# One expert fewer in wide form, residual rows written in one piece, and the overflow branch moved to the end of a one-core decoder layer

## The chip, the cores and the metric

The kernel runs on one core of a Trainium2 chip. The metric is device time in microseconds of one execution; 812.87 us is the median of three runs of the kernel before (807.72, 812.87 and 814.02). The trace is that of one profiled execution.

## The reference

One layer of a decoder: 512 positions of width 1024. Three mixers (dilated window attention, a chunked state-space mixer, attention into 256 memory tokens) share an input projection, and their outputs go through `w_out`. Then a LayerNorm and a mixture of 16 experts, two for each position, and a second LayerNorm:

```python
x = _layer_norm(ALPHA * x + y, ln1_g[l], ln1_b[l])
y = _moe(x, w_router, b_router, w_gate[l], w_up[l], w_down[l])
x = _layer_norm(ALPHA * x + y, ln2_g[l], ln2_b[l])

def _moe(...):
    ...                        # top 2 experts of the best group of four; gates: 512 x 16
    for e in range(N_EXPERTS):
        h = jax.nn.silu(x @ w_gate[e]) * (x @ w_up[e])
        out = out + gates[..., e:e + 1] * (h @ w_down[e])
```

Each expert has three matrices of 1024 x 1024 in float32, 4.19 MB each, 201 MB in all.

## The kernel before

**Front.** Projections, the three mixers, `w_out` and the first LayerNorm run until about 285 us of the profiled execution. A planner (`Plan`, with `add` and `chain`) gets operations with an engine, a cost, what they depend on and a priority, and emits them in an order. The normed rows stay in four tiles `res`, one for each 128 positions.

**Experts.** The experts are computed on gathered rows only. Two kinds of places exist: HEAVY has room for 96 rows in three groups of 32, LIGHT for 64 rows in one group. Places 0 and 1 belong to experts 0 and 1; the other experts are sorted by their number of rows on the chip (`sort`), the larger ones into the HEAVY places. `PROG` is the order of the 16 places; two in a row form a pair, whose rows are gathered together by one-hot matmuls (`gather`, line 1316; for the first pair `gather_early`, line 1380) into `X`. An expert is a product with `w_gate`, a Silu on ACT, a product with `w_up`, a multiplication on VectorE, transposes (`turn`), and a product with `w_down`; down of one expert stands behind gate and up of the next. `gemm` (line 1438) loads a matrix as 8 tiles of 128 x 1024 (512 KB), each from `slot()`. A HEAVY product uses its tile in 12 matmuls as the program lists them, which the trace records as 24, a LIGHT one in 2, recorded as 4. Four accumulator banks `acc` are cycled; a HEAVY product takes two, a LIGHT one one.

**Buffers and queues.** `turns` is the order in which `slot()` hands out 33 tile buffers: raws 8, rawm 4, raw2 4, quarters 6, his 4, los 4, loopw 3, and so on again. In the trace raw stands for several of these pools, and X for two of the quarters. All weights are issued on SP's DMA queue in program order; a load waits until its buffer is no longer read and until an earlier load of the ring has landed.

**Result rows.** `xbuf` is a 512 x 1024 array in memory. It holds first the rows that the second LayerNorm adds to: SP writes the scaled bias `b1b` into it (line 988), and `residue` multiplies `res` by the scaled gain (line 1122) and adds it with accumulating DMAs on POOL's queue (line 1123). `down` then scales its result by the gate and adds it to rows of `xbuf` with an indirect accumulating DMA for each group (line 1496), 32 in all. The last two experts' down product stays on chip.

**Overflow and tail.** Rows beyond a place's room are counted in `nlefti`. `rest()` (lines 1515 to 1577) reads this count on every engine (line 1517) and, where it is above zero, runs a loop that computes them with its own weight loads into `loopw`. It stands between the last expert's up product and the tail. The tail (from 1699 on): the down weights of the last pair as 32 halves of 256 KB (line 1713), the second LayerNorm's two rows (1715), `rest()`, the transposes (1739), the product of the last pair (1749), its spreading over positions (1763), the sums with the rows read from `xbuf` (read at 1729, added at 1767), statistics, normalization (1803, 1807) and stores (1808).

Of the kernel before, what the change touches and what calls it, by code (L numbers as in the profile page):

```python
# [43 lines left out]
FIX, N_HEAVY = 2, 9  # L44
PROG = [0, 1, 2, 3, 9, 10, 4, 5, 11, 12, 6, 7, 8, 13, 14, 15]
# [62 lines left out]
def kernel(ctx, tc, x, mem, w_in, w_out, rel_bias, conv_w, conv_b, dt_bias, a_log, d_skip,  # L108
# [623 lines left out]
    plan = Plan(dict(raw=NR, hi=4, lo=4, pj=2, sc=2, tr=2, av=2, A=2, B=2, Lk=2, tb=2, mx=4, den=4, pv=2, t3=2, rT=2, rq=2, rs1=2, left=2, lt=2, xt=2,  # L732
# [243 lines left out]

    raw2 = ctx.enter_context(tc.tile_pool(name="raw2", bufs=NR4, reuse_waits="tile"))
    b1b = raw2.tile([128, 1024], F32, name="raw")
    nc.sync.dma_start(b1b, bass.AP(tensor=ln1_b[0].tensor, offset=ln1_b[0].offset, ap=[[0, 128], [1, 1024]]))
# [5 lines left out]

    def biased():
        for b in range(4):
            nc.sync.dma_start(xbuf[b * 128:(b + 1) * 128, :], b1b)
    add("SP", 0.1, biased, scale[:1])
# [46 lines left out]
    def logits_of(b, prio, deps):  # L1036

        def out():
            got["lt", b] = p2.tile([128, 128], F32, name="lt")
# [217 lines left out]
    cycle = NR * [raws] + NR2 * [rawm] + NR4 * [raw2] + NQ * ["quarter"] + 4 * [his] + 4 * [los] + NR3 * ["loopw"]  # L1257
    turns = 24 * cycle

    def slot(loop=False):  # L1260

        pool = "loopw" if loop else turns[cnt[0]]
        n, cnt[0] = turns[:cnt[0]].count(pool), cnt[0] + (not loop)
# [104 lines left out]
    def gather_early():  # L1368
# [35 lines left out]
    for b in range(4):  # L1404
        add("DVE", 0.5, lambda b=b: [place(b, pos1[:, b, z:z + 1], (HEAVY, HEAVY), z, REACH[b]) for z in range(2)], [put_at[b]], (), 402.0)

# [108 lines left out]
    def rest():  # L1515

        n_more = nc.values_load(nlefti[0:1, 0:1], min_val=0, max_val=16 * NJ)
        with tc.If(n_more > 0):
            with tc.For_i(0, n_more, 1):
# [58 lines left out]
                down(HEAVY, wrows[2], rows, turn(HEAVY, hh, X[:, :, HEAVY.slots:]), idx, gt)  # L1578

    def sort():  # L1580
# [3 lines left out]
        pc = mis("ps_c")  # L1584
        for b in range(4):
            T.matmul(pc[:, 0:16], oneb, sel[:, b, :], start=b == 0, stop=b == 3, skip_group_check=True)
        key, rank, numf = wide("key", 16), wide("rank", 16), wide("numf", 16)
        sq = pxt.tile([128, 512], F32, name="xt")[:, :256].rearrange("p (a b) -> p a b", a=16)
        V.scalar_tensor_tensor(key, pc[:, 0:16], 16.0, tie, op0=OP.mult, op1=OP.add)
        V.tensor_tensor(sq, key[:, None, :].to_broadcast([128, 16, 16]), key[:, :, None].to_broadcast([128, 16, 16]), op=OP.is_gt)  # L1590
        red(rank, sq)
        V.tensor_tensor(sq, rank[:, None, :].to_broadcast([128, 16, 16]), i16[:, :, None].to_broadcast([128, 16, 16]), op=OP.is_equal)
        V.tensor_tensor(sq, sq, i16[:, None, :].to_broadcast([128, 16, 16]), op=OP.mult)
        red(numf, sq)
        num = pf.tile([128, 16], I32, name="num")
        V.tensor_copy(num, numf)
# [52 lines left out]
        return num, numf, pos2, rem, nlefti  # L1649
# [11 lines left out]

    for i, j in enumerate(PROG):
# [17 lines left out]
        to = kind, e, idx[:, c:c + kind.groups], gt[:, c:c + kind.groups]  # L1680
        prev = lambda hh=hh, kind=kind: turn(kind, hh), lambda H, to=to: down(to[0], (w_down, to[1]), None, H, *to[2:])

        if z == 0 and i < 14:
            for b in range(4):
                for y in range(2):
                    j2 = PROG[i + 2 + y]
                    place(b, posx[:, b, j2:j2 + 1], pair_of(i + 2), y)
        elif i < 14:
# [6 lines left out]
    PT = px.tile([128, 512], F32R)  # L1695
# [7 lines left out]
    for e_ in range(2):  # L1703
        V.tensor_copy(gate2[e_ * 64:(e_ + 1) * 64], gt[e_ * 64:(e_ + 1) * 64, e_:e_ + 1])
# [137 lines left out]


# [28 lines left out]
```

## Time and profile before

| | us |
|---|---|
| runs | 807.72, 812.87, 814.02 |
| profiled execution, its own time | 808.93 |
| its span | 807.2 |
| TensorE busy | 769.5 (95%) |
| VectorE / ACT / POOL busy | 315.0 / 222.9 / 93.3 |
| DMA moved | 245.65 MB, mean 304 GB/s over the span |

The span is read by stages: the front until 285 us, the experts until 761 us, the tail from there. The shares of the whole span mix them; the rows further down are each of one stage. A row of a window gives each engine's busy time, with the number of instructions in brackets, then TensorE's granted clock as a share of full, the DMA engines' busy share and what they moved. A row of waits gives the total, the number of waits and the longest. A row of a timeline gives start and length of a run of instructions, and in square brackets the idle time before it with what ended it.

### The profile page before, as it was taken

Reading aid. Unit: us, or ns where it says so; the run is one execution under the profiler, and the core shown is the slowest. Engines: PE = TensorE matmul, PEld = TensorE weight load, DVE = VectorE, ACT = ScalarE, POOL = GpSimd, SP = SyncE. Lnnn points to the kernel's source line nnn. Section 1 sums busy time; section 2 is a strip of 40 time slices with the busy share of each in tenths; the row PEclk is TensorE's granted clock in tenths of the full one; section 3 lists DMA queues with packets and bytes.
Section 4 is the critical chain, followed back from the end, with each engine's and each line's share of the span. In section 5 each row is a group of like instructions: output and inputs, shape, how many; then the busy total and the mean of one; then the engine's idle time right before and its main releaser. Section 6 shows DMA issues by size and latency. Waiting matters only on the chain. (4 is left out here: it accounts for less than half of the span.)

```text
span 807.2 us, 20819 instructions
## 1 busy us (share of the span) xinstructions
PE 769.5 (95%) x8497; PEld 488.8 (61%) x8497; DVE 315.0 (39%) x1028; ACT 222.9 (28%) x449; POOL 93.3 (12%) x158
## 2 busy tenths in 40 slices
PE   7999999999999899999999999999999999999790
PEld 6897799787777666666654464654454556443240
DVE  5688877988957883020010020010200001010018
ACT  5667653577744330010010010010110000010112
POOL 5201200111010010010111100011100001102000
PEclk9999999999999889999999999999999999999986
DMA  8932555722574979999999999999999999999992
GB/s 290 299 95 64 80 57 75 256 79 79 189 274 162 349 201 363 417 404 412 403 405 400 393 403 399 413 404 395 400 393 413 408 404 406 408 390 406 335 343 106
DMA packets 94004, 245.65 MB, mean 304 GB/s; under 512 B 11154, under 2 KB 33240, under 8 KB 93904
## 3 DMA queue, kind: packets, MB, share of 16 engines
q1 hardware_dynamic: 86336, 232.31, 74.6%
q0 software_dynamic: 7568, 11.95, 9.0%
q8 instruction: 69, 1.13, 0.5%
q14 instruction: 31, 0.25, 0.1%
HBM read 231.46 MB, written 13.76 MB: 304 GB/s over the span
## 5 line engine op out<-in xcount | busy, mean ns | idle before, releaser
L1438 PE MATMUL acc<-raw,X 128*32 128x256 f32 (+1 forms) x2548 | 182.6, 400 | 0.0
L1438 PEld LDWEIGHTS acc<-raw,X 128*32 128x32 f32 (+1 forms) x2548 | 88.5, 113 | 76.5 <-issue 21.4
L1496 POOL DMA_INDIRECT xbuf<-y,idx x32 | 49.6, 1549 | 403.0 <-ACT y L1512 250.1
L1438 PE MATMUL acc<-raw,H 128*32 128x256 f32 (+1 forms) x1228 | 79.4, 389 | 0.0
L1512 ACT ACTIVATE y<-acc,gt 128x256 f32<-128x256 f32 (+1 forms) x23 | 11.2, 520 | 221.5 <-PE acc L1438 156.3
L1472 DVE TENSOR_TENSOR hh<-hh,acc 128x512 f32<-128x512 f32 (+1 forms) x24 | 13.4, 585 | 124.6 <-PE acc L1438 124.6
L1438 PEld LDWEIGHTS acc<-raw,H 128*32 128x32 f32 (+1 forms) x1228 | 40.6, 111 | 31.2 <-issue 6.3
L1462 ACT ACTIVATE hh<-acc 128x512 f32<-128x512 f32 (+1 forms) x25 | 12.1, 519 | 135.6 <-PE acc L1438 135.6
L1316 PEld LDWEIGHTS <-c 128*128 128x128 bf16 x768 | 31.9, 98 | 28.2 <-issue 28.1
L298 PE MATMUL pj<-hi,xh 128*128 128x256 f32 (+2 forms) x144 | 48.2, 335 | 0.4 <-ACT xh L897 0.4
L299 PE MATMUL pj<-lo,xh 128*128 128x256 f32 (+2 forms) x144 | 46.6, 324 | 0.0
L300 PE MATMUL pj<-hi,xl 128*128 128x256 f32 (+2 forms) x144 | 46.3, 321 | 0.1
L298 PE MATMUL pj<-xh,hi 128*128 128x512 f32 x112 | 45.6, 407 | 0.8 <-DVE pl L619 0.6
L300 PE MATMUL pj<-xh,lo 128*128 128x512 f32 x112 | 44.4, 397 | 0.0
L299 PE MATMUL pj<-xl,hi 128*128 128x512 f32 x112 | 44.3, 395 | 0.0
L1328 DVE TENSOR_SCALAR X<-ps_g,vcol 128x192 f32<-128x192 f32 (+2 forms) x28 | 12.1, 443 | 77.2 <-ACT X L1326 34.0
L1510 DVE TENSOR_SCALAR y<-acc,gt 128x256 f32<-128x256 f32 x9 | 4.4, 484 | 88.8 <-ACT y L1512 88.8
L1316 PE MATMUL ps_g<-P,c 128*128 128x64 bf16 (+2 forms) x768 | 38.1, 202 | 0.0
L1438 PE MATMUL acc<-quarters,X 128*32 128x256 f32 (+1 forms) x460 | 35.7, 404 | 0.0
L1438 PE MATMUL acc<-hi,X 128*32 128x256 f32 (+1 forms) x324 | 34.3, 437 | 0.0
L1438 PE MATMUL acc<-lo,X 128*32 128x256 f32 (+1 forms) x396 | 33.3, 413 | 0.0
L298 PEld LDWEIGHTS pj<-hi,xh 128*128 128x128 f32 x144 | 27.1, 189 | 3.0 <-issue 1.0
(480 smaller groups left out, 1273.6 us busy)
## 6 DMA issues: line engine op xcount, KB each, us to landing
raw<-in_w_up_dram SPq DMA_DIRECT2D x78, 512.0 KB
raw<-in_w_gate_dram SPq DMA_DIRECT2D x74, 512.0 KB
raw<-in_w_down_dram SPq DMA_DIRECT2D x62, 512.0 KB
raw<-in_w_in_dram SPq DMA_DIRECT2D x22, 512.0 KB
hi<-in_w_gate_dram SPq DMA_DIRECT2D x17, 512.0 KB
quarters<-in_w_gate_dram SPq DMA_DIRECT2D x15, 512.0 KB
quarters<-in_w_up_dram SPq DMA_DIRECT2D x15, 512.0 KB
lo<-in_w_down_dram SPq DMA_DIRECT2D x15, 512.0 KB
```

The costliest lines, as they stand in the source:

```text
L298: T.matmul(p, ah, bh, start=first, stop=False, skip_group_check=True)
L299: T.matmul(p, ah, bl, start=False, stop=False, skip_group_check=True)
L300: T.matmul(p, al, bh, start=False, stop=last, skip_group_check=True)
L1316: T.matmul(o, src[:, b, k * 128:(k + 1) * 128], i, start=fresh, stop=b == 3 and src is c3, skip_group_check=True)
L1328: V.tensor_scalar(X[:, k, :n], src, gT[:, k:k + 1], bT[:, k:k + 1], op0=OP.mult, op1=OP.add)
L1438: T.matmul(out_of(kind, a, t, g), L(k, g), r[:, t * kind.chunk:(t + 1) * kind.chunk], start=k == 0 and g * kind.chunk % 512 == 0, stop=k = ...
L1462: S.activation(hh[:, c], a[:, :c.stop - c.start], AF.Silu)
L1472: V.tensor_mul(hh[:, c], hh[:, c], a[:, :c.stop - c.start])
L1496: nc.gpsimd.indirect_dma_start(out=xbuf.rearrange("t (n c) -> (t n) c", n=kind.tiles), out_offset=bass.IndirectOffsetOnAxis(ap=idx[:, g:g ...
L1510: V.tensor_scalar(y[:, c], src, gt[:, g:g + 1], None, op0=OP.mult)
L1512: S.activation(y[:, c], src, AF.Copy, scale=gt[:, g:g + 1])
```

## The change

- `N_HEAVY` is 8 in place of 9, and `PROG` is rewritten so that the seventh pair is (12, 13), both LIGHT, where it was (8, 13), HEAVY and LIGHT. The other pairs keep their kinds.
- The bias is loaded by POOL into a tile of its own. `residue` multiplies by the gain and adds the bias on VectorE, and the row goes to `xbuf` as a plain write on ACT's DMA queue. SP's four bias writes and POOL's four accumulating writes are gone.
- `turns` begins with raws and rawm only; raw2, quarters, his, los, raws, rawm, loopw follow in this order: loopw is used first by the 42nd to 44th tile, where it was the 31st to 33rd.
- Of the sort, the counts and ranks (7 VectorE operations, 4 matmuls) move into the plan ahead of the first gate; the rest, and the first pair's targets, stand behind the second gate, not the first.
- The matmuls of `gather_early` get another cost and priority.
- `rest()` stands behind everything, with `again()`, which repeats the last steps if rows were left over. The loop uses tile buffers that hold no weights by then.
- The reads of `xbuf` are issued before the second LayerNorm's rows. `PT` is a tile from `slot()`.

```diff
-FIX, N_HEAVY = 2, 9
-PROG = [0, 1, 2, 3, 9, 10, 4, 5, 11, 12, 6, 7, 8, 13, 14, 15]
+FIX, N_HEAVY = 2, 8
+PROG = [0, 1, 2, 3, 8, 9, 4, 5, 10, 11, 6, 7, 12, 13, 14, 15]
...
+    b1b = bcast(ln1_b[0], 1024, "b1b", po)
     raw2 = ctx.enter_context(tc.tile_pool(name="raw2", bufs=NR4, reuse_waits="tile"))
-    b1b = raw2.tile([128, 1024], F32, name="raw")
-    nc.sync.dma_start(b1b, bass.AP(tensor=ln1_b[0].tensor, offset=ln1_b[0].offset, ap=[[0, 128], [1, 1024]]))
...
-    def biased():
-        for b in range(4):
-            nc.sync.dma_start(xbuf[b * 128:(b + 1) * 128, :], b1b)
-    add("SP", 0.1, biased, scale[:1])
...
     def residue(b):
 
-        return [*[("DVE", 0.66, lambda c=c: V.tensor_mul(res[b][:, c], res[b][:, c], g1b[:, c])) for c in (slice(0, 512), slice(512, 1024))],
-                ("Pool", 1.0, lambda: nc.gpsimd.dma_start(xbuf[b * 128:(b + 1) * 128, :], res[b], accum_op=OP.add))]
+        cs = (slice(0, 512), slice(512, 1024))
+        return [*[("DVE", 0.61, lambda f=f, g=g, c=c: f(res[b][:, c], res[b][:, c], g[:, c]))
+                  for f, g in ((V.tensor_mul, g1b), (V.tensor_add, b1b)) for c in cs],
+                ("ACT", 0.1, lambda: nc.scalar.dma_start(xbuf[b * 128:(b + 1) * 128, :], res[b]))]
...
-    cycle = NR * [raws] + NR2 * [rawm] + NR4 * [raw2] + NQ * ["quarter"] + 4 * [his] + 4 * [los] + NR3 * ["loopw"]
-    turns = 24 * cycle
+    turns = NR * [raws] + NR2 * [rawm] + 24 * (NR4 * [raw2] + NQ * ["quarter"] + 4 * [his] + 4 * [los] + NR * [raws] + NR2 * [rawm] + NR3 * ["loopw"])
...
-                d = [add("PE", 0.45, lambda b=b, i=i: mm(b, i), [*d, put_at[b], normed[b, i // 2]], use, 140.0 + i)]
+                d = [add("PE", 0.8, lambda b=b, i=i: mm(b, i), [*d, put_at[b], normed[b, i // 2]], use, 270.0 + i)]
...
+    tot = add("PE", 0.2, totals, list(put_at.values()), [("tr", "tot"), ("rT", "sq")], 320.0)
+    tot = add("DVE", 0.17, lambda: V.scalar_tensor_tensor(key, got["tot"][:, 0:16], 16.0, tie, op0=OP.mult, op1=OP.add), [tot],
+              [("tr", "tot")], 299.0)
+    chain("DVE", 299.0, [tot], [
...
-        if i == 0:
-            num, numf, pos2, rem, nlefti = sort()
-        if z == 0:
-            idx, gt = targets(kinds, lambda b, e: meta[:, b, PROG[i + e], :])
+        if i == 1:
+            pos2, rem, nlefti = sort()
+        if i == 1 or z == 0 and i > 0:
+            aim[i // 2] = targets(kinds, lambda b, e: meta[:, b, PROG[i // 2 * 2 + e], :])
+        if i == 1:
+            next_places(0)
...
-    PT = px.tile([128, 512], F32R)
+    PT = slot()[:, :512].bitcast(F32R)
...
-    for t, src in ((g2b, ln2_g[0]), (b2b, ln2_b[0])):
-        nc.sync.dma_start(t, bass.AP(tensor=src.tensor, offset=src.offset, ap=[[0, 128], [1, 1024]]))
-    rest()
+    loop_slots += rr
...
     for n in range(2):
         for b in range(4):
             rr_in[n, b] = comes(rr[b][:, CH[n]], xbuf[b * 128:(b + 1) * 128, CH[n]], 262144)
+    for t, src in ((g2b, ln2_g[0]), (b2b, ln2_b[0])):
+        comes(t, bass.AP(tensor=src.tensor, offset=src.offset, ap=[[0, 128], [1, 1024]]), 524288)
...
         plan.run()
 
+    def again():
+
+        for b in range(4):
+            r = rr[b]
+            nc.sync.dma_start(r, xbuf[b * 128:(b + 1) * 128, :])
...
+    rest()
```

Three places show how the instructions now stand. On ACT, between the front's last copies and the first Silu (line 1462 before, 1481 now; `hh` is the Silu's result), by the difference:

```order
 L1326 ACTIVATE X<-pj,vcol 128x192 x2
+L1108 ACTIVATE c_2909<-left 128x512
 L1326 ACTIVATE X<-sc,vcol 128x192 x2
-L1115 ACTIVATE c_2909<-left 128x512 x6
-L1462 ACT_TABLE_LOAD
...
+L1108 ACTIVATE c_2909<-left 128x512 x5
+L1118 DMA xbuf<-res_2950 128x1024
+L1118 DMA xbuf<-res_2949 128x1024
+L1118 DMA xbuf<-res_2948 128x1024
+L1118 DMA xbuf<-res_2947 128x1024
+L1481 ACT_TABLE_LOAD
```

The four writes of rows now stand in ACT's queue ahead of the table load and of the first Silu.

On TensorE, between the last expert's up product (the last acc rows; line 1438 before, 1457 now) and the transposes of the tail, before:

```order
L1438 MATMUL acc<-lo,X 64x512 x8
L1438 MATMUL acc<-raw,X 64x512 x16
L1517 TENSOR_LOAD nlefti
L1518 COMPARE_AND_BRANCH
L1519 COMPARE_AND_BRANCH
...
L1518 UNCONDITIONAL_BRANCH
L1739 MATMUL ps_h<-ident,hh 128x128 x4
L1749 MATMUL acc<-raw,H 64x512
```

and now:

```order
L1457 MATMUL acc<-lo,X 64x512 x8
L1457 MATMUL acc<-raw,X 64x512 x16
L1753 MATMUL ps_h<-ident,hh 128x128 x4
L1763 MATMUL acc<-raw,H 64x512
...
L1777 MATMUL ps_y<-yl,raw 128x512
L1536 TENSOR_LOAD nlefti
L1537 COMPARE_AND_BRANCH
```

The transposes follow the up product directly; the count and the branch stand behind TensorE's last matmul.

On SP, behind the last half of the down weights, before:

```order
L1713 DMA X<-in_w_down_dram 128x512
L1715 DMA X<-in_ln_g_dram 128x1024
L1715 DMA hi<-in_ln_b_dram 128x1024
L1517 TENSOR_LOAD nlefti
L1518 COMPARE_AND_BRANCH
...
L1729 DMA hi<-xbuf 128x512
L1729 DMA lo<-xbuf 128x512 x3
...
L1808 DMA out_dram<-lo 128x512 x6
```

and now:

```order
L1727 DMA X<-in_w_down_dram 128x512
L1741 DMA lo<-xbuf 128x512 x8
L1741 DMA hi<-in_ln_g_dram 128x1024
L1741 DMA hi<-in_ln_b_dram 128x1024
L1536 TENSOR_LOAD nlefti
L1536 ISA x2
L1822 DMA out_dram<-lo 128x512 x8
L1537 COMPARE_AND_BRANCH
```

The reads of `xbuf` follow the weights, the branch follows the stores.

## Rows read from the trace of the kernel before

**Rows 1.** Windows, the whole core: busy time by engine, clock, DMA.

```profile
core 0: us, PE busy (x) PEld busy (x) DVE busy (x) ACT busy (x) POOL busy (x), PEclk, DMA share, GB/s
312.00:760.00 448.00, 447.41 (x6326) 233.87 (x6320) 47.23 (x163) 44.86 (x99) 49.56 (x32) 1.00 1.03 402
...
765.00:770.00 5.00, 2.92 (x8) 1.35 (x10) 0.00 (x0) 0.00 (x0) 0.00 (x0) 0.50 0.99 354
775.00:780.00 5.00, 5.00 (x26) 2.16 (x24) 0.75 (x1) 2.17 (x3) 0.00 (x0) 1.00 0.92 324
780.00:785.00 5.00, 5.00 (x24) 2.65 (x21) 1.06 (x3) 0.69 (x1) 0.00 (x0) 1.00 1.02 372
785.00:790.00 5.00, 2.95 (x10) 1.18 (x8) 5.00 (x24) 3.98 (x10) 0.00 (x0) 1.00 0.25 95
```

**Rows 2.** Waits of SP's queue, 305 to 745 us: total, times, longest.

```profile
SPq L1280 <- DMA raw<-in_w_gate_dram: 48.7, 63, 2.2
...
SPq L1280 <- PE acc L1438: 21.2, 75, 1.2
```

**Rows 3.** Windows of the tile acc: one heavy and one light product.

```profile
357.80:368.30 10.50, 10.50 (x196) 6.36 (x200) 0.34 (x1) 0.00 (x0) 1.00 1.03 405
732.70:739.70 7.00, 7.00 (x36) 2.41 (x34) 0.00 (x0) 0.60 (x1) 1.00 1.04 416
```

**Rows 4.** Timeline of TensorE, end of the experts and start of the tail.

```profile
755.56 5.75 PE L1438 MATMUL acc<-raw,X 128*64 128x512 f32 x26
762.84 0.63 PE L1739 MATMUL ps_h<-ident,hh 128*128 128x128 f32 x4 [1.53 <-DVEq L1518]
767.08 1.11 PE L1749 MATMUL acc<-raw,H 128*64 128x512 f32 x1 [3.62 <-issue]
```

**Rows 5.** Chain of waits: start, length, what.

```profile
763.48 3.60 issue
```

**Rows 6.** Line 1518, the branch: shortest, median, longest ns; first and last start.

```profile
L1518 ACTq COMPARE_BRANCH  x1: 50/50/50, 755.0 to 755.0; - x1
...
L1518 PEldq COMPARE_BRANCH  x1: 4846/4846/4846, 757.5 to 757.5; - x1
```

**Rows 7.** Timeline of VectorE, the first sum of the tail.

```profile
783.94 0.69 DVE L1767 SCALAR_TENSOR_TENSOR hi<-ps_y,hi 128x512 f32<-128x512 f32 x1 [6.05 <-DMA hi<-xbuf]
```

**Rows 8.** Timeline of the span's end, the last store.

```profile
803.98 0.33 SPq L1808 DMA_DIRECT2D out_dram<-lo  x1
```

**Rows 9.** Page, costliest groups: gather matmuls, busy us and mean ns of one.

```profile
L1316 PE MATMUL ps_g<-P,c 128*128 128x64 bf16 (+2 forms) x768 | 38.1, 202 | 0.0
```

**Rows 10.** Page, DMA queues: packets, MB, share of 16 engines' span.

```profile
q0 software_dynamic: 7568, 11.95, 9.0%
```

**Rows 11.** Line 1123, the accumulating writes of rows.

```profile
L1123 POOL DMA_DIRECT2D xbuf<-res x4: 848/879/1117, 291.9 to 299.1; - x4
...
DMA to landing us min/median/max: 8.2/9.5/13.0
```

**Rows 12.** Line 1122, the multiplications of `residue`.

```profile
L1122 DVE TENSOR_TENSOR res<-res,g1b x8: 683/689/691, 287.9 to 298.1; 128x512 f32<-128x512 f32 x8
```

**Rows 13.** Timeline of ACT, the first Silu.

```profile
295.85 1.28 ACT L1462 ACT_TABLE_LOAD   x1 [1.22 <-DVE c L1116]
297.15 0.87 ACT L1462 ACTIVATE hh<-acc 128x512 f32<-128x512 f32 x2
```

**Rows 14.** Timeline of TensorE, start of the first gate product.

```profile
285.33 5.00 PE L1438 MATMUL acc<-raw,X 128*32 128x256 f32 x76
```

**Rows 15.** Waits of SP's queue, 270 to 305 us.

```profile
SPq L1280 <- DMA xbuf<-res: 8.1, 1, 8.1
```

**Rows 16.** Timeline of SP's queue near 400 us.

```profile
401.27 2.33 SPq L1280 DMA_DIRECT2D raw<-in_w_gate_dram  x2
```

**Rows 17.** Timeline of TensorE near 400 us.

```profile
397.79 2.56 PE L1438 MATMUL acc<-raw,X 128*32 128x256 f32 x44
```

**Rows 18.** Waits of SP's queue, 380 to 435 us.

```profile
SPq L1280 <- PE acc L1438: 4.9, 14, 1.2
```

More of the change, by code (lines that the diff above doesn't have):

```diff
@@ L731 @@
     at4 = es3.enter_context(tc.tile_pool(name="at4", bufs=4, reuse_waits="tile"))
-    plan = Plan(dict(raw=NR, hi=4, lo=4, pj=2, sc=2, tr=2, av=2, A=2, B=2, Lk=2, tb=2, mx=4, den=4, pv=2, t3=2, rT=2, rq=2, rs1=2, left=2, lt=2, xt=2,
+    plan = Plan(dict(raw=NR, hi=4, lo=4, pj=2, sc=2, tr=2, av=2, A=2, B=2, Lk=2, tb=2, mx=4, den=4, pv=2, t3=2, rT=2, rq=2, rs1=2, left=2, lt=1, xt=2,
                      **{f"{t}{j}": 2 for t in "phl" for j in range(4)}))
@@ L1038, in out @@
         def out():
-            got["lt", b] = p2.tile([128, 128], F32, name="lt")
+            got["lt", b] = p2.tile([128, 128], F32, name="lt", bufs=1)
             S.activation(got["lt", b], lgT[:, b * 128:(b + 1) * 128], AF.Copy)
@@ L1255 @@
     cnt = [0]
-    cycle = NR * [raws] + NR2 * [rawm] + NR4 * [raw2] + NQ * ["quarter"] + 4 * [his] + 4 * [los] + NR3 * ["loopw"]
-    turns = 24 * cycle
+    turns = NR * [raws] + NR2 * [rawm] + 24 * (NR4 * [raw2] + NQ * ["quarter"] + 4 * [his] + 4 * [los] + NR * [raws] + NR2 * [rawm] + NR3 * ["loopw"])
+    loop_slots = []
     def slot(loop=False):
-        pool = "loopw" if loop else turns[cnt[0]]
-        n, cnt[0] = turns[:cnt[0]].count(pool), cnt[0] + (not loop)
+        if loop:
+            loop_slots.append(loop_slots.pop(0))
+            return loop_slots[-1]
+        pool = turns[cnt[0]]
+        n, cnt[0] = turns[:cnt[0]].count(pool), cnt[0] + 1
         if pool == "quarter":
@@ L1578, in rest @@
                 down(HEAVY, wrows[2], rows, turn(HEAVY, hh, X[:, :, HEAVY.slots:]), idx, gt)
+            again()
     def sort():
@@ L1583, in sort @@
         red = lambda o, i: V.tensor_reduce(o, i, axis=AX.X, op=OP.add)
[L1584 to L1596, printed above, removed]
         rb, ib = rank[:, None, :].to_broadcast([128, 4, 16]), i16[:, None, :].to_broadcast([128, 4, 16])
@@ L1648, in sort @@
         V.tensor_copy(nlefti, nleft)
-        return num, numf, pos2, rem, nlefti
+        return pos2, rem, nlefti
     posx = pf.tile([128, 4, 16], F32)
@@ L1660, in pair_of, with next_places @@
         return tuple(kind_of(j) for j in PROG[i // 2 * 2:i // 2 * 2 + 2])
+    def next_places(i):
+        for b in range(4):
+            for y in range(2):
+                j2 = PROG[i + 2 + y]
+                place(b, posx[:, b, j2:j2 + 1], pair_of(i + 2), y)
+    aim = {}
     for i, j in enumerate(PROG):
@@ L1679 @@
         c = before(kinds, z)[0] // 128
[L1680 to L1688, printed above, removed]
+        to = kind, e, i // 2, slice(c, c + kind.groups)
+        prev = (lambda hh=hh, kind=kind: turn(kind, hh),
+                lambda H, to=to: down(to[0], (w_down, to[1]), None, H, *[t[:, to[3]] for t in aim[to[2]]]))
+        if z == 0 and 0 < i < 14:
+            next_places(i)
+        elif z == 1 and i < 14:
             gather(pair_of(i + 1))
@@ L1703 @@
     for e_ in range(2):
-        V.tensor_copy(gate2[e_ * 64:(e_ + 1) * 64], gt[e_ * 64:(e_ + 1) * 64, e_:e_ + 1])
+        V.tensor_copy(gate2[e_ * 64:(e_ + 1) * 64], aim[7][1][e_ * 64:(e_ + 1) * 64, e_:e_ + 1])
     wd = [[slot() for _ in range(2)] for _ in range(8)]
@@ L1841 @@
         plan.run()
+    def again():
+        for b in range(4):
+            r = rr[b]
+            nc.sync.dma_start(r, xbuf[b * 128:(b + 1) * 128, :])
+            st, mv = pe.tile([128, 2, 6], F32, name="st", bufs=1), pe.tile([128, 2], F32, name="mv", bufs=1)
+            for n in range(2):
+                p = mis("ps_y")
+                for y in (yh, yl):
+                    T.matmul(p, PT[:, b * 128:(b + 1) * 128], y[:, CH[n]], start=y is yh, stop=y is yl)
+                V.tensor_add(r[:, CH[n]], r[:, CH[n]], p)
+                V.bn_stats(st[:, n, :], r[:, CH[n]])
+            V.bn_aggr(mv, st)
+            rs = rsqrt1(pe, mv[:, 1:2], LN_EPS)
+            V.tensor_scalar(mv[:, 0:1], mv[:, 0:1], -1.0, None, op0=OP.mult)
+            V.scalar_tensor_tensor(r, r, mv[:, 0:1], g2b, op0=OP.add, op1=OP.mult)
+            V.scalar_tensor_tensor(r, r, rs, b2b, op0=OP.mult, op1=OP.add)
+            nc.sync.dma_start(out[b * 128:(b + 1) * 128, :], r)
+    rest()
 _INS = ['x', 'mem', 'w_in', 'w_out', 'rel_bias', 'conv_w', 'conv_b', 'dt_bias', 'a_log', 'd_skip',
```

13 lines of the change are left out of this document (added).

## The prediction

> **What bounds the kernel now.** I read the windows first. Between 312 and 760 us TensorE is busy 447.41 of 448 us, and the DMA engines have a share of 1.03 at 402 GB/s [rows 1]: two resources are full, and the engine table cannot say which one holds the other. The second view, what SP's queue waits for, decides. From 305 to 745 us its loads wait for an earlier landing of their own ring in most of the lines (48.7 us behind gate tiles alone, 63 times), and for TensorE to free a buffer only 21.2 us in all, 75 times and never over 1.2 us [rows 2]. So the stream of weights sets the pace of the experts, with TensorE just behind it. One matrix is 8 tiles of 512 KB, 4.19 MB, which at 402 GB/s are 10.4 us. A heavy expert's product over it takes 10.5 us of TensorE (192 matmuls) and a light one's 7.0 (32) [rows 3]: heavy products keep step with the stream, light ones gain on it.
>
> The third view is the chain of waits. It ends in the tail: TensorE finishes the last expert's up product at 761.31, idles 1.53 us behind the branch on the overflow count, transposes for 0.63 and idles again [rows 4], 3.60 us for nothing but "issue" [rows 5]. TensorE's own COMPARE_BRANCH of that If took 4846 ns, ACT's 50 ns [rows 6]. [...] VectorE starts its final sums at 783.94, having waited 6.05 us, and SP issues the last store 20.0 us later, at 803.98 [rows 7, 8].
>
> The profiled execution took 808.93 us; the sum is made against it. The median of the runs, 812.87, lies 3.94 above, and that is added at the end.
>
> **The change part by part.**
>
> *Place 8 light instead of heavy.* Three products become light: 3 x (10.5 - 7.0) = 10.5 us less on TensorE [rows 3]; 96 of 768 gather matmuls go, 38.1 x 96/768 = 4.8 us [rows 9]. The bytes stay. Since light products are already shorter than their load, these 15.3 us turn into waiting for weights: 0 on the stream. The overflow loop would cost a load of 24 tiles, some 31 us, per turn; by the reference's routing of these inputs the largest expert that becomes light has 64 tokens, and a light expert has 64 slots, so its body stays unused.
>
> *Scatters.* 32 become 30: three of 128 rows of 1 KB go, one of 128 rows of 2 KB comes. The software queue's 7,568 packets took 9.0% of 16 engines' span, 72.6 us, 9.6 ns each [rows 10]: by packets (256 fewer) 2.5 us less on the stream, by bytes (as for 128) 1.2. I take 1.2, since the one that comes is wide.
>
> *Residual rows.* Four accumulating writes that took 9.5 us to land [rows 11] and four writes of the bias go; four plain writes on ACT's queue come. SP's queue stood 8.1 us behind one of the accumulates [rows 15]: that is the most the stream can gain at its start. VectorE pays eight more 128x512 operations, 8 x 0.689 = 5.5 us, and ahead of them the seven of the moved sort, at most half as wide: an estimate of 7 x 0.689/2 = 2.4 us. The last residual operation ended at 298.8 [rows 12] and would end near 306.7. Behind these writes on ACT stand the first Silu's table load, 1.28 us, and the Silu, 0.87 for its two halves [rows 13]: the first half is through near 308.5. The first gate's two accumulators are needed again by the second gate (four banks, two for a heavy product), which follows two products after the first gate's start at 285.33 [rows 14], near 307. TensorE waits 0 to 2 us, I take 1.0.
>
> *How much of the 8.1 us survives.* At 401.27 SP issues the next gate's first load [rows 16], and the buffer it refills was read until about 400.35 [rows 17]; in 380 to 435 us SP waits 14 times for TensorE [rows 18]. A stream that comes earlier meets buffers still in use there: 0.9 us can pass, not 8.1, and TensorE's wait of 1.0 above takes that back: 0. The rest of TensorE's work up to there is the same in both programs, so the buffers come free no sooner.
>
> *The three late buffers.* Used first at the 42nd tile, not the 31st: three tiles (3 x 1.3 = 3.9 us of stream) wait for the first gate. Cover: the early gain that is cut off at 400 us anyway. 0, at most +3.9 if that cover is absent.
>
> *The sort, the early gather's priority, the targets of pair 0.* Same matmuls, one product later; nothing late waits for them. 0, within 1 us.
>
> *The branch to the end.* The stretches of 1.53 and 3.60 us go out of the middle [rows 4, 5]. But the last weights then decide. After 775 us 5 x 324 + 5 x 372 + 5 x 95 GB/s, 3.95 MB, moved [rows 1]; of these 3.15 are LayerNorm's two rows (2 x 0.52) and the eight reads of rows (8 x 0.26), so 0.81 MB of down weights were open: the last lands near 775 + 2.5 = 777.5. With the stream 1.2 earlier: 776.3. TensorE's last two halves (four matmuls of 0.365 us at half clock, 8 in 2.92 us [rows 1], and their release) end some 2 us later, 778.3; VectorE starts 0.7 later (one sum's length), 779.0 in place of 783.94: **-4.9 us**. The reads of rows follow the weights directly, 0.70 to 0.81 us apart at 372 to 324 GB/s, and VectorE's sums take 0.69 each, so they keep step; LayerNorm's rows are needed only after them.
>
> *The branch at the end.* Every engine now loads the count and jumps over the loop behind its last work. TensorE, ACT and POOL have been done for long; SP and VectorE have not. Price: between 0.05 us (ACT) and 4.85 + 3.60 (TensorE) [rows 5, 6]. These two have short code there, as ACT, and the last stores land meanwhile: **+0.5**. [...]
>
> Sum: -4.9 + 0.5 = -4.4: 804.5 in place of 808.93, so **808.5** against the median of 812.87 (0.5% less).
>
> **The rivals.** Within 1% (8.1 us, 804.7 to 821.0) a measurement of this kernel cannot be told from no change.
>
> - *The early gain carries through:* TensorE is itself earlier at 400 us (its first gate starts sooner without the sort's vector work beside it), and all 8.1 us pass: 808.5 - 8.1 = 800.4. For it: the length of that wait [rows 15]. Against: the buffer that came free only at 400.35 [rows 17]. 14%.
> - *TensorE was the bound:* the 15.3 us come off the end: 797.6. For it: its 447.41 of 448 us. Against: the landings in SP's queue [rows 2]. 6%.
> - *Half clock eats the tail's gain:* once light products wait for every tile, the granted clock falls as it did after the idle stretches before 765 us. The last up product then takes 14.0 us beside a load of 10.4, and the 64 matmuls of the last product 64 x 0.365 = 23.4: it ends some 3.5 us later, 812.0. 16%. [...]
> - *The jump at the end is a slow one* on VectorE or SP: one fetch, 8.4 us in place of 0.5, gives 816.4 (6%). **Slower:** load 0.5, two jumps of 4.85 one after the other and the 3.60 of issue make 13.8, 808.5 + 13.3 = 821.8; it decides from 13.0 us on. For it: VectorE skips as much of the loop's body as the others, and two unconditional branches stand behind it. Against: ACT's 50 ns. 8%.
>
> My forecast has 50%, with a range of its own of 805 (scatters 2.5, no wait at 307, 0.8 us behind the last landing) to 813.4 (the late buffers' 3.9, TensorE waiting 2).
>
> **How the numbers follow.** Faster by over 1%: 14 + 6 and about 13 of the forecast's lower edge, 33%. Slower: the double jump, 8%. Within: 59%. The range leaves out the full TensorE case, the double jump and slivers: 799.5 to 816.5.
>
> **What would show it.** SP's row for the wait behind xbuf<-res is gone, and its waits for TensorE rise in 340 to 410 us while the loads behind 435 come at the same time as before, less a microsecond or so. TensorE waits for weights in the light products from about 700 us on. No "issue" of 3.60 stands before the last product, and VectorE's first sum starts near 779. Behind the last store, VectorE's or SP's branch shows its price. The forecast is wrong if the loads behind 435 us come several us sooner, if TensorE stands idle long near 307 us, or if the granted clock stays at 0.5 behind 745 us.

## The result, and the profile after

The changed kernel takes 805.58 us (median of 13, 801.59 to 809.55), the kernel before, run beside it, 810.59 (median of 13). The ratio is 0.9942, with an interval of 0.9926 to 0.9959: 4.7 us less by the ratio, 5.0 by the medians, no change by more than 1%. 4.4 us had been forecast. A second comparison, on another chip (the control below), gave 0.9924 (0.9900 to 0.9948).

The profiled execution of the changed kernel has a span of 799.9 us, against 807.2. With 801.59 us it is the fastest of its 13, so its 7.3 us of gain are some 2.5 more than the medians show; what follows splits these 7.3.

SP's waits from 305 to 745 us, to be held against [rows 2] (total, times, longest):

```profile
SPq L1280 <- PE acc L1457: 63.0, 112, 4.6
SPq L1280 <- DMA raw<-in_w_gate_dram: 41.1, 56, 1.8
...
SPq L1280 <- DMA xbuf<-res: 5.8, 1, 5.8
```

The wait for TensorE to free buffers has tripled, from 21.2 us to 63.0: the stream starts earlier and is cut, as forecast. The wait behind xbuf<-res was forecast to go; it is 5.8 in place of 8.1 [rows 15], and comes later: the plain writes still stand where SP's next loads wait for them. The same row from 345 to 380 us alone:

```profile
SPq L1280 <- PE acc L1457: 21.0, 22, 4.6
```

SP's queue at the first load of a gate matrix that has 112 tiles of expert weights ahead of it (called the 112th load here), which answers to [rows 16], and at the first half load of the last down matrices:

```profile
401.23 2.92 SPq L1280 DMA_DIRECT2D raw<-in_w_gate_dram  x3
...
743.20 0.33 SPq L1727 DMA_DIRECT2D raw<-in_w_down_dram  x1
```

The 112th load is issued at the same time as before (401.27), but not behind the same wait. SP's waits from 398 to 404 us, before and then now:

```profile
SPq L1280 <- DMA raw<-in_w_up_dram: 1.4, 2, 0.7
SPq L1280 <- DMA raw<-in_w_down_dram: 1.4, 1, 1.4
```

```profile
SPq L1280 <- PE acc L1457: 2.9, 4, 0.7
```

Before, SP waited there for earlier loads to land; now it waits for TensorE to free buffers, and the loads ahead have landed sooner. From issue to landing, those into `raw` from 395 to 402 us took:

```profile
DMA to landing us min/median/max: 5.4/5.9/6.1
```

On the page of this run the medians of the three largest groups of weight loads are 9.9, 10.2 and 9.9. The trace of the kernel before has no landings of SP's loads. In the kernel before, the first half load was issued at 746.13, here 2.9 us earlier.

ACT around the first Silu, beside [rows 13], and what TensorE waited for between 285 and 320 us:

```profile
298.31 6.95 ACTq L1118 DMA_DIRECT2D xbuf<-res  x4
306.56 1.28 ACT L1481 ACT_TABLE_LOAD   x1 [10.01 <-DMA xbuf<-res]
307.85 0.87 ACT L1481 ACTIVATE hh<-acc 128x512 f32<-128x512 f32 x2
```

```profile
PE acc L1457 <- ACT hh L1481: 2.7, 1, 2.7
```

The table load does not only stand behind the issue of the writes, which ends at 305.26 (298.31 + 6.95). It waits until 306.56 for the landing of one: the Silu's result lies where a row of `res` lay, and the row must have been read out. The trace has the second of the four writes landing at 306.47.

TensorE at the end of the last up product, which answers to [rows 4]: each tile is waited for, then the transposes and the last product follow.

```profile
751.52 1.08 PE L1457 MATMUL acc<-raw,X 128*64 128x512 f32 x4 [0.20 <-DMA raw<-in_w_up_dram]
752.77 1.08 PE L1457 MATMUL acc<-raw,X 128*64 128x512 f32 x4 [0.17 <-DMA raw<-in_w_up_dram]
754.71 0.66 PE L1753 MATMUL ps_h<-ident,hh 128*128 128x128 f32 x4 [0.86 <-DVE hh L1754]
755.29 1.07 PE L1763 MATMUL acc<-raw,H 128*64 128x512 f32 x2
```

No 3.60 of issue, and no half clock, as the window shows (clock, DMA share, GB/s at the end):

```profile
745.00:775.00 30.00, 27.85 (x98) 8.64 (x99) 1.44 (x2) 3.13 (x5) 0.00 (x0) 1.00 1.00 375
```

VectorE's first sum and SP's last stores, beside [rows 7, 8]:

```profile
775.32 0.69 DVE L1781 SCALAR_TENSOR_TENSOR lo<-ps_y,lo 128x512 f32<-128x512 f32 x1 [9.71 <-PE ps_y L1777]
```

```profile
785.99 9.73 SPq L1822 DMA_DIRECT2D out_dram<-lo  x8
```

The first sum waited for DMA before and waits for TensorE now. The last store's issue ends at 795.72, 20.4 us after the first sum's start, as before (804.31 - 783.94 = 20.4), and the span ends 4.2 us later, where it was 2.9: 1.3 us more. The branch at the end by engines:

```profile
L1537 PEldq COMPARE_BRANCH  x1: 3780/3780/3780, 779.8 to 779.8; - x1
...
L1537 DVEq COMPARE_BRANCH  x1: 76/76/76, 795.5 to 795.5; - x1
L1537 SPq COMPARE_BRANCH  x1: 53/53/53, 795.8 to 795.8; - x1
```

TensorE's jump is nearly as slow as it was (3780 ns for the 4846 of [rows 6]), but long over by the end. On VectorE and SP it is short; ahead of it stands VectorE's load of the count:

```profile
L1536 DVEq TENSOR_LOAD <-nlefti x1: 822/822/822, 794.6 to 794.6; - x1
```

The split of the 7.3 us, from profile to profile: 2.9 until the first half load is issued (746.13 to 743.20), 5.7 from there to the first sum (37.8 us to 32.1), 0 to the last store, and 1.3 given back behind it.

### The profile page after: what moved, and what is told of

Read it like the earlier page. It is cut to its first block, busy times and chain, and to the rows that moved or that the text cites. A ratio compares the mean times of both kernels' runs of the same rounds, so it can differ in the third digit from the quotient of the medians.

```text
span 799.9 us, 19636 instructions
## 1 busy us (share of the span) xinstructions
PE 760.2 (95%) x7911; PEld 473.1 (59%) x7911; DVE 318.1 (40%) x1032; ACT 222.6 (28%) x446; POOL 87.2 (11%) x153
## 4 chain that ended last, share of the span: by engine, by line
PE 80%; DVE 9%; DMA 5%; ACT 3%; issue 1%; SPq 0%; ACTq 0%; DVEq 0%
PE acc L1457 48%; PE pj L298 5%; PE pj L299 5%; PE pj L300 5%; PE ps_g L1316 4%; PE acc L1763 2%; DMA raw<-in_w_up_dram 1%; PE ps_h L1502 1%; DMA raw<-in_x_dram 1%; DVE res L1116 1%; PE sc L278 1%; DVE lo L1821 1%; PE av L285 1%; PE tr L851 1%; DMA X<-in_w_down_dram 1%
## 5 line engine op out<-in xcount | busy, mean ns | idle before, releaser
L1515 POOL DMA_INDIRECT xbuf<-y,idx x30 | 46.5, 1551 | 423.0 <-ACT y L1531 283.1
L1316 PEld LDWEIGHTS <-c 128*128 128x128 bf16 x672 | 30.1, 98 | 28.6 <-issue 28.6
L1316 PE MATMUL ps_g<-P,c 128*128 128x64 bf16 (+1 forms) x672 | 37.2, 207 | 0.0
L1328 DVE TENSOR_SCALAR X<-ps_g,vcol 128x128 f32<-128x128 f32 (+1 forms) x28 | 12.0, 438 | 61.9 <-PE acc L1457 32.7
L1457 PE MATMUL acc<-quarters,X 128*32 128x256 f32 (+1 forms) x380 | 34.0, 419 | 2.7 <-ACT hh L1481 2.7
L1457 PE MATMUL acc<-hi,X 128*32 128x256 f32 (+1 forms) x244 | 32.3, 469 | 0.0
## 6 DMA issues: line engine op xcount, KB each, us to landing
raw<-in_w_gate_dram SPq DMA_DIRECT2D x74, 512.0 KB, 10.2
```

The source lines that it names most:

```text
L1316: T.matmul(o, src[:, b, k * 128:(k + 1) * 128], i, start=fresh, stop=b == 3 and src is c3, skip_group_check=True)
L1328: V.tensor_scalar(X[:, k, :n], src, gT[:, k:k + 1], bT[:, k:k + 1], op0=OP.mult, op1=OP.add)
L1457: T.matmul(out_of(kind, a, t, g), L(k, g), r[:, t * kind.chunk:(t + 1) * kind.chunk], start=k == 0 and g * kind.chunk % 512 == 0, stop=k = ...
L1515: nc.gpsimd.indirect_dma_start(out=xbuf.rearrange("t (n c) -> (t n) c", n=kind.tiles), out_offset=bass.IndirectOffsetOnAxis(ap=idx[:, g:g ...
```

## The experiments

Twelve kernels, in three groups of four; each was also timed against the kernel before. The theory of the first groups (A) is that of the forecast; the last group works with A2, corrected by what came before. The columns of the table are from the timelines of one profiled execution each: TensorE's wait before the second gate, the issue of the 112th tile's load and of the first half load, and the start of the first sum. The wait of the last row is that of the sort's matmuls, which stand ahead of the second gate there.

| kernel | wait | 112th load | first half | first sum | ratio to before, interval |
|---|---|---|---|---|---|
| before | 0 | 401.27 | 746.13 | 783.94 | 1 |
| changed | 2.7 | 401.23 | 743.20 | 775.32 | 0.9942, 0.9926 to 0.9959 |
| changed, control | 2.9 | 401.93 | 743.92 | 776.30 | 0.9924, 0.9900 to 0.9948 |
| before, no branch | 0 | 402.52 | 746.99 | 782.52 | 0.9955, 0.9938 to 0.9973 |
| before, eight heavy | 0 | 400.78 | 745.80 | 781.01 | 0.9967, 0.9946 to 0.9988 |
| changed, no branch | 1.2 | 400.92 | 744.47 | 777.00 | 0.9887, 0.9855 to 0.9919 |
| changed, nine heavy | 3.5 | 406.21 | 748.65 | 783.64 | 0.9967, 0.9947 to 0.9986 |
| changed, reads undone | 3.6 | 404.25 | 745.59 | 781.09 | 0.9972, 0.9954 to 0.9989 |
| changed, rows undone | 0 | 401.49 | 745.85 | 777.92 | 0.9897, 0.9870 to 0.9923 |
| changed, rows by POOL | 2.2 | 402.20 | 744.07 | 776.20 | 0.9907, 0.9882 to 0.9933 |
| changed, turns undone | 0.7 | 398.87 | 740.21 | 773.05 | 0.9877, 0.9854 to 0.9900 |
| changed, turns undone, rows by POOL | 1.6 | 399.87 | 741.08 | 774.33 | 0.9896, 0.9866 to 0.9926 |
| changed, turns and rows undone | 0 | 399.90 | 744.06 | 775.90 | 0.9911, 0.9886 to 0.9936 |
| changed, early gather undone | 6.9 | 409.44 | 750.90 | 784.41 | 1.0009, 0.9989 to 1.0028 |

One thing is not in the table and differs between these profiles: the first gate, ahead of all this, starts at 284.89 in the changed kernel and from 283.84 (the control) to 287.71 (nine heavy) in the others. In the eight profiles with the rows written directly and the gather as in the change, the 112th load is issued when TensorE frees its buffer, 87.3 to 87.4 us after the second gate has used its first four tiles. So the start of the first gate, the wait, and the granted clock behind the wait (0.57 to 1.00 from 310 to 315 us in these profiles) add up to the time of this load.

**The tail, from the kernel before.**

```diff
 # e1_before_no_branch
-    rest()
```

> The kernel before without rest(): the overflow count is still made, but the branch on it and the loop behind it are left out (they compute nothing on these inputs). Theory A (the last weights' landing sets the end as soon as nothing stalls TensorE in the tail): the idle 1.53 and 3.60 us before the last product go, that product runs at full clock, VectorE's first sum comes at 779 to 780 in place of 783.94, so about 4 us less than the kernel before, ratio 0.995. Theory B (the change's gain is the TensorE work that the eighth light expert saves): at most 1 us less, ratio 0.999.

```diff
 # e4_before_eight_heavy
-FIX, N_HEAVY = 2, 9
-PROG = [0, 1, 2, 3, 9, 10, 4, 5, 11, 12, 6, 7, 8, 13, 14, 15]
+FIX, N_HEAVY = 2, 8
+PROG = [0, 1, 2, 3, 8, 9, 4, 5, 10, 11, 6, 7, 12, 13, 14, 15]
```

> The kernel before with N_HEAVY = 8 and the new order of places, nothing else. Theory A: TensorE ends the last up product near 753, the branch's 1.5 and 3.6 us pass while the down weights still land, and the last product ends with the last landing: about 4 us less than the kernel before, ratio 0.995, the same 4 us that the branch alone gives. Theory C (starved TensorE falls to half clock and gives it back): ratio 0.999 to 1.000.

Both ratios are about as theory A said. Theory B (the saved TensorE work is the gain) falls with the first, whose interval ends at 0.9973. Theory C asks 0.999 and falls with the second only barely (0.9988): TensorE's granted clock was 0.94 there from 745 to 775 us, where the changed kernel has 1.00, and behind the 5.1 us of the branch the first three matmuls of the last product took 1.06 to 1.11 us, later ones 0.59. From the first half load to the first sum they need 35.5 and 35.2 us, where the kernel before needs 37.8 and the changed one 32.1. What stopped both at the same place, theory A had not named. First the kernel without the branch, then the one with eight heavy places, first sums on VectorE:

```profile
782.52 0.69 DVE L1766 SCALAR_TENSOR_TENSOR hi<-ps_y,hi 128x512 f32<-128x512 f32 x1 [9.43 <-DMA lo<-xbuf]
```

```profile
781.01 0.69 DVE L1767 SCALAR_TENSOR_TENSOR hi<-ps_y,hi 128x512 f32<-128x512 f32 x1 [9.38 <-DMA lo<-xbuf]
```

Both wait for the reads of `xbuf`, behind LayerNorm's two rows. So the order of these reads became a suspect of its own.

```diff
 # u_reads_undone, from the changed kernel
+    for t, src in ((g2b, ln2_g[0]), (b2b, ln2_b[0])):
+        comes(t, ..., 524288)
     for n in range(2):
         for b in range(4):
             rr_in[n, b] = comes(rr[b][:, CH[n]], xbuf[...], 262144)
-    for t, src in ((g2b, ln2_g[0]), (b2b, ln2_b[0])):
-        comes(t, ..., 524288)
```

> The changed kernel with the second LayerNorm's two rows loaded ahead of the reads of xbuf, as before. Theory A2 (after the runs so far: in the kernel before, VectorE's first sum waited for the reads of xbuf, which stood behind 1.05 MB of rows that are needed later): the reads land 2.6 to 3 us later, the first sum waits for them, and the end comes 2 to 3 us later than in the changed kernel: 0.996 to 0.997 of the kernel before. Rival (TensorE's last product decides, the reads are covered): the same as the changed kernel, 0.993.

```profile
781.09 0.69 DVE L1781 SCALAR_TENSOR_TENSOR lo<-ps_y,lo 128x512 f32<-128x512 f32 x1 [12.72 <-DMA lo<-xbuf]
```

35.5 us from the first half load to the first sum, 3.4 more than in the changed kernel, and the time is 0.9972: as A2 said. With eight heavy places, the order of the reads decides between 35 and 32. The profile's end is later by more than these 3.4 us: its first half load is 2.4 us later too, after a wait of 3.6 us near 307 and a granted clock of 0.74 from 305 to 310 and 0.57 from 310 to 315.

```diff
 # e3_after_nine_heavy, from the changed kernel
-FIX, N_HEAVY = 2, 8
-PROG = [0, 1, 2, 3, 8, 9, 4, 5, 10, 11, 6, 7, 12, 13, 14, 15]
+FIX, N_HEAVY = 2, 9
+PROG = [0, 1, 2, 3, 9, 10, 4, 5, 11, 12, 6, 7, 8, 13, 14, 15]
```

> The changed kernel with N_HEAVY = 9 and the order of places of before. Theory A: TensorE reaches the last up product's end near 761 again in place of 754, its last product takes 14 us at full clock and ends near 777, some 2 to 3 us later than in the changed kernel (ratio to the kernel before 0.997). If TensorE's saved work were the whole gain (theory B): as slow as the kernel before, ratio 1.000. If the stream alone sets the end: no slower than the changed kernel, 0.994.

0.9967, the ratio of theory A. In its profile TensorE starts the last product only at 768.16, and the stretch takes 35.0 us, so the eighth light place is needed too. But the stretch is one part: its first half load is also 5.4 us later than the changed kernel's. 2.8 of these come from the front, whose first gate starts at 287.71 in place of 284.89; 0.8 from a longer wait (3.5 us near 310), and the 1.3 left over stand beside a granted clock of 0.66 from 310 to 315. The size is right in part for reasons that were not in the expectation.

```diff
 # e2_after_no_branch, from the changed kernel
-    rest()
```

> The changed kernel without rest(): branch, loop and the repeated last steps left out. It prices the branch behind the last store. Forecast: 0.5 us less than the changed kernel. Rival (a slow jump on VectorE or SP): 3 to 8 us less.

Behind the last store the span ends 2.9 us later (800.3 less 787.64 + 9.73), 1.3 less than with the branch: between the 0.5 of the forecast and the rival's 3. The time is 0.9887, some 3 to 4 us below the changed kernel, on four executions; the branch's own stretch explains 1.3 of it. The rest is open. Its wait before the second gate was 1.2, not 2.7 to 2.9, but its first gate started 1.2 us later than the changed kernel's (286.08), and its first sum is no earlier (777.00).

**The start of the stream.**

> The changed kernel itself, as a control on the chip of the three runs beside it: 0.994 of the kernel before (0.992 to 0.997). By theory A its spread comes from the first expert: in a slower execution TensorE waits longer than the 2.7 us of its profile before the second gate.

The control repeats the gain. Its wait is longer by 0.2, and here the clock falls, which in the changed kernel's profile it did not (its first gate starts 1.1 us earlier, so the 112th load is only 0.7 later):

```profile
305.00:310.00 5.00, 2.35 (x24) 1.19 (x28) 2.81 (x14) 2.15 (x3) 0.00 (x0) 0.74 0.95 325
310.00:315.00 5.00, 5.00 (x90) 2.68 (x84) 1.25 (x4) 0.00 (x0) 0.00 (x0) 0.92 1.03 407
```

```diff
 # t_turns_undone, from the changed kernel
-    turns = NR * [raws] + NR2 * [rawm] + 24 * (NR4 * [raw2] + ... + NR * [raws] + NR2 * [rawm] + NR3 * ["loopw"])
+    turns = 24 * (NR * [raws] + NR2 * [rawm] + NR4 * [raw2] + ... + NR3 * ["loopw"])
```

> The changed kernel with the buffers' turns as before (loopw used by the 31st to 33rd tile). Theory A: three loads go out before the first gate, but the stream meets TensorE near 400 us either way: the same as the changed kernel within 1 us, 0.993 to 0.996. Rival (late buffers give the stream its lead): 3 to 4 us later, 0.998.

Neither came: 0.9877, 3.7 us below the control beside it (800.21 against 803.91; the two intervals meet at 0.9900). The late turns cost time. The profile says where:

```profile
296.94 6.97 ACTq L1118 DMA_DIRECT2D xbuf<-res  x4
304.18 1.28 ACT L1481 ACT_TABLE_LOAD   x1 [9.01 <-PE acc L1457]
305.47 0.87 ACT L1481 ACTIVATE hh<-acc 128x512 f32<-128x512 f32 x2
```

```profile
398.87 0.34 SPq L1280 DMA_DIRECT2D raw<-in_w_gate_dram  x1
```

The row names TensorE, but the first gate had ended long before: the table load follows ACT's last issue (296.94 + 6.97 = 303.91) by 0.3 us. In the control ACT's last issue ends at the same time (303.92), and the table load starts 1.5 us later (305.71). Here it waits for no row, TensorE's wait is 0.7, and everything behind it is 3 to 4 us earlier than in the control: the 112th load, the first half load (740.21), the first sum. One profile speaks against the turns as the only cause: the changed kernel without the branch has the late turns, and its table load starts 0.1 us after ACT's last issue.

```diff
 # r_rows_undone, from the changed kernel: residue, the bias and its writes as before
-        return [*[("DVE", 0.61, lambda f=f, g=g, c=c: f(res[b][:, c], res[b][:, c], g[:, c]))
-                  for f, g in ((V.tensor_mul, g1b), (V.tensor_add, b1b)) for c in cs],
-                ("ACT", 0.1, lambda: nc.scalar.dma_start(xbuf[b * 128:(b + 1) * 128, :], res[b]))]
+        return [*[("DVE", 0.66, lambda c=c: V.tensor_mul(...)) for c in (slice(0, 512), slice(512, 1024))],
+                ("Pool", 1.0, lambda: nc.gpsimd.dma_start(xbuf[b * 128:(b + 1) * 128, :], res[b], accum_op=OP.add))]
...
+    add("SP", 0.1, biased, scale[:1])
```

> The changed kernel with the residual rows as before: bias written by SP, accumulating writes on POOL's queue, two VectorE operations a row in place of four. Theory A (what the first Silu waits for delays TensorE, and TensorE's freeing of buffers near 400 us sets the stream from there on): TensorE's 2.7 us wait before the second gate is gone, SP's wait behind xbuf<-res is 8 us again, the load at the 112th tile is issued 2 to 3 us earlier than in the changed kernel, and the end comes 2 to 4 us earlier: ratio to the kernel before 0.990 to 0.992. Rival (the plain rows' faster start of the stream is worth something at the end): 3 to 5 us later than the changed kernel, 0.998.

The time is as A said, but not by A's road. TensorE's wait is gone; SP's wait behind xbuf<-res does not come back, and the 112th load is not earlier (401.49). SP waits for TensorE 20.5 us from 305 to 745, as in the kernel before: this stream is not cut at all, it is late by itself. Its first half load is the latest of its group but its first sum comes 32.1 us later. Against the control the 1.9 us of the medians (802.03 and 803.91) lie within the intervals: writing the rows directly gained nothing that shows here.

```diff
 # r_rows_pool_first, from the changed kernel
-                ("ACT", 0.1, lambda: nc.scalar.dma_start(xbuf[...], res[b]))]
+                ("Pool", 1.0, lambda: nc.gpsimd.dma_start(xbuf[...], res[b]))]
...
-            ends = [add(eng, cost, step, ends, (), 405.0 + 10 * b, 0.12, 0.3)]
+            ends = [add(eng, cost, step, ends, (), 405.0 + 10 * (1, 0, 2, 3)[b], 0.12, 0.3)]
```

> The changed kernel with its four plain row writes on POOL's queue in place of ACT's, and with the row whose buffer the first Silu's result takes over written first. Theory A: ACT's table load waits for nothing but the first gate, TensorE's 2.7 us wait is gone, SP's wait behind xbuf<-res too, and the end comes 2 to 4 us earlier than in the changed kernel: 0.990 to 0.992. Rival (only the stream's own rate counts, the wait is covered): the same as the changed kernel, 0.994.

The wait is 2.2, not 0. The Silu still waits for the landing of its row. This row's write is issued 3.1 us earlier than in the changed kernel (298.19 for 301.32), but takes 7.5 us to land in place of 5.2, and the table load starts 0.1 us after it (305.82): the slower landing took most of what the earlier issue gained. The clock fell here too (granted 0.81 from 305 to 310, 0.85 from 310 to 315).

Turns and rows both undone, by the two edits above:

> The changed kernel with the buffers' turns and the residual rows both as before. Theory A2: no wait before the second gate, but the stream starts late behind the accumulating writes and is not cut by TensorE near 400 us; its first half load of the last down matrices is issued some 5 us later than with the turns alone undone: 0.990 to 0.992 of the kernel before. Rival (the rows written directly are worth nothing): 0.988.

0.9911, as A2 said. TensorE does not wait at all, its first half load is at 744.06, 3.9 us after that of the turns alone undone. With this the two effects stand apart. With the turns as before, the direct writes bring the first half load 3.9 us forward (the ratios, 0.9877 and 0.9911, differ by 2.8 us, but their intervals overlap); with the late turns their landing holds the first Silu, and they show no gain.

The turns undone, with the rows written by POOL:

> The changed kernel with the buffers' turns as before, its row writes on POOL's queue, and the row first whose buffer the first Silu's result takes over. Theory A2 (the end follows TensorE's time near 400 us, which the wait before the second gate delays): that wait, 0.7 us with the turns alone undone, goes to 0 to 0.3, and the end comes 0 to 0.7 us earlier: 0.987 to 0.988 of the kernel before. Rival (POOL's writes land later than ACT's, so the Silu waits longer): 0.990 to 0.992.

0.9896, between the two; the interval holds both values, so the time settles nothing. The wait does: 1.6, more than the 0.7 with ACT's writes, as the rival said. The turns alone undone remain the best version run that still handles an overflow, better than both kernels.

```diff
 # u_early_undone, from the changed kernel
-    add("PE", 0.8, lambda b=b, i=i: mm(b, i), [...], use, 270.0 + i)
+    add("PE", 0.45, lambda b=b, i=i: mm(b, i), [...], use, 140.0 + i)
```

> The changed kernel with cost and priority of the early gather's matmuls as before. Theory A2: the first gate starts within 1 us of the changed kernel, and the end with it: 0.992 to 0.995 of the kernel before. Rival (the early gather in its old place delays the router or the first gate): 2 us or more later, 0.996.

The rival, and three times its size: 1.0009, the whole gain gone. What TensorE waited for from 285 to 320 us, what VectorE waited for ahead of the sort, and TensorE's clock:

```profile
PE ps_c L1627 <- DVE selp L1616: 6.9, 1, 6.9
```

```profile
312.75 0.23 DVE L1607 TENSOR_TENSOR t<-first,rank 128x64 f32<-128x64 f32 x1 [5.53 <-DMA xbuf<-res]
```

```profile
310.00:315.00 5.00, 0.47 (x11) 0.45 (x15) 1.99 (x11) 2.15 (x3) 0.00 (x0) 0.53 1.02 415
315.00:320.00 5.00, 5.00 (x52) 2.25 (x51) 3.29 (x19) 0.00 (x0) 0.00 (x0) 0.50 1.02 419
```

The first gate starts 1.9 us later (286.75 in place of 284.89), which lies within the spread of the other profiles. The sort's matmuls, which the changed kernel has behind the second gate (319.00), now stand ahead of it. TensorE waits 6.9 us there for VectorE, which is busy with the rows until 307 and then waits 5.5 us itself for the landing of a row's write, and TensorE then runs at half clock. It is the landing of the rows again, with another engine waiting for it; in the changed kernel VectorE waits for it too (2.8 us), but TensorE does not stand behind that. The 112th load is 8.2 us later, and the first half load 7.7.

## Why the prediction was right, and where its steps failed

The forecast of 0.5% less, within 1%, held, and so did its frame: the stream decides; what is gained at its start is cut by TensorE near 400 us; the tail gives most of the gain. That the number came so near is in part luck. The sum was built on one profile, and from profile to profile its gains came out larger and make 7.3 us, not 4.4; the medians show less, as the changed kernel's profile is its fastest execution. The forecast time of 808.5 was made against a median of three runs (812.87); 805.58 lies near the lower edge of its range of 805 to 813.4, and 4.4 below 810.59 would be 806.2. Step by step:

- *The stream gains 1.2 us* (nothing at the start, 1.2 by scatters): 2.9 in the profiles. The scatters gave nothing that shows: the kernel before with eight heavy places needs 345.0 us from the 112th load to the first half load, as without (344.9). The 2.9 are the start's. Here the mechanism was wrong. "0.9 us can pass", taken back by TensorE's wait, is right for the issue of the 112th load (0.04 us earlier); the step took this for all that passes. Before, the buffer was free at 400.35, and SP issued the load when an earlier one had landed. Now TensorE frees the buffer just before the issue, and the loads ahead have landed sooner (5.4 to 6.1 us after their issue there, where the medians of the three largest groups are 9.9 to 10.2; that they took longer in the kernel before is inferred from SP's waits). The lead shows behind it: the programs in which TensorE releases the 112th load need 341.2 to 343.6 us from there to the first half load, the others (before, the two kernels made from it, and the two with the rows undone), in which a landing does, 344.2 to 345.0. The direct rows and this wait always come together in these runs, so none separates them.
- *TensorE waits 1.0 us (0 to 2) near 307*: 2.7 to 2.9, and up to 3.6 in other profiles. The Silu's first half was forecast through near 308.5 and was, at 308.45, but by two errors that cancel: VectorE's rows end at 304.90, not 306.7, and the landing, for which the table load waits until 306.56, was not priced at all, only the issue of the writes. TensorE itself was ready at 305.82, not near 307, and so waits longer. Later times follow this wait (0.7 to 3.6 between kernels that differ in little), the clock behind it, and the start of the first gate: together they move the 112th load from 398.87 to 406.21.
- *The late buffers cost 0 to 3.9*: near the upper end, 3.7 by the medians, but not for the reason given. Beside direct rows they do not leave the stream late; in the profiles they put weight loads beside the row writes, whose landing the Silu then waits for. That the traffic does it is an inference from two profiles; no run changed the traffic alone, and the kernel without the branch had late buffers and no such wait for a landing.
- *Sort, early gather and targets cost nothing*: no run speaks against it for the kernel as it is, but it is wrong as a bound of 1 us. With the sort behind the second gate, the gather's priority decides where its matmuls land, and that is worth 5 to 7 us.
- *The branch out of the middle, -4.9*: this holds the stream's 1.2, so the tail alone was to give 3.7. It gave 5.7, for one reason more, and the first sum starts at 775.32, not 779.0. The forecast let the last landing of weights decide, and called the reads of rows no limit. They were the limit in the kernel before: the [6.05 <-DMA hi<-xbuf] of [rows 7] says so, and the forecast read this row only for its start. The light place and the order of reads are both needed for the 32 us: with either of them undone it is 35. The branch back in the middle beside these two was not tried.
- *The branch at the end, +0.5*: +1.3, and the slow jump did not come. Only TensorE's jump is slow (3780 ns), and there it is now hidden; ACT's took 45, VectorE's 76 and SP's 53 ns. What TensorE's jump waits for was not shown. No run shows the "one fetch" of the rival at 816.4 either, whose 8.4 us were an estimate from [rows 5, 6]; in its place the runs showed these 76 and 53 ns.
- *Half clock in the starved light products*: it did not come; the granted clock stays at 1.00 from 745 to 775. These waits are 0.2 to 0.9 us each. A lower clock came near 310 instead, behind the Silu's wait, and not in every profile: granted 0.57 to 0.92 from 310 to 315 in four of them, 1.00 in the changed kernel.
- *The double jump*, the case for slower, was not there. Of the 8.1 us of *The early gain carries through* 2.9 passed, but not by its road: TensorE is not earlier at 400 us.

Of the signs that it named, the waits for TensorE rose, and the 3.60 us of issue and the half clock behind 745 us stayed away. TensorE waits for weights only from 743 us on (2.5 us in 8 waits), not from 700. Two signs of being wrong came in part: the loads behind 435 us come 1.7 to 3.0 us sooner (the 200th at 518.92 for 520.59, the 300th at 651.22 for 654.21), and TensorE stands idle 2.7 us near 307.

Two things stay open. The last down loads moved at 375 GB/s in the changed kernel and at 348 in the one before (745 to 775 us), and no run explains it: eight heavy places in the kernel before give 350, nine in the changed one 333. And the spread of the changed kernel's executions (8 us) is put down here to the wait near 307 and the clock behind it from single profiles; no timed execution shows its own wait, and the kernel before, which has no such wait, spreads over 6.3 us.

## What to carry to other kernels

When a stream is cut by buffers further on, an issue at the same time need not mean the same state. Here the 112th load was issued at 401.23 for 401.27, but the loads ahead of it had landed 5.4 to 6.1 us after their issue, where the medians of the three largest groups are 9.9 to 10.2: look at what SP waited for ahead of such an issue. The buffer of a row was free for the Silu not when its write was issued (301.32) but when it had landed (306.47, the table load starting at 306.56): where the next tile takes a buffer's place, price the landing, and name who waits for it. And read the releaser in the last wait of the tail. In the kernel before it was a DMA [rows 7], and in the changed one, between the first half load and the first sum, the order of the last reads was worth 3.4 us (35.5 for 32.1), the light place ahead of them 2.9 (35.0 for 32.1).

## What the runs showed of the hardware

A write of 512 KB from ACT's queue took 4.7 to 6.9 us to land, 5.1 in the median of four (the changed kernel), the same from POOL's queue 6.5 to 7.5, 7.3 in the median (rows by POOL), and POOL's accumulating one 9.5 [rows 11]. TensorE's granted clock stayed at 1.00 after a wait of 2.7 us (the changed kernel, 305 to 315) and fell after one of 2.9 in the same place (the control: 0.74 in 305 to 310, 0.92 in 310 to 315) and one of 2.2 (rows by POOL: 0.81 and 0.85 in the same windows): the length of this wait alone does not tell. The branch on the count took TensorE 3780 and 4846 ns in two kernels, ACT, VectorE and SP 45 to 76 ns.
